# Hybrid encoder: the first two tiles of the first feed-forward layer, fed and ordered differently

## Chip, cores, metric

The kernel runs on one core of one Trainium2 chip. The metric is the device time of one execution in microseconds, the median of the runs. TensorE multiplies, ScalarE, VectorE and GpSimd work on elements, SP issues most transfers; ScalarE and GpSimd issue some too.

## The reference, cut to what matters

Two layers of an encoder over x of 512 tokens x 1024 features. Each layer is a half-step feed-forward block, a mixer with three kinds of attention, and a second feed-forward block; a norm follows at the end. All data is float32. The change touches only the very beginning: the first block's normalised input, multiplied by the gate and up weights.

```
h = rms_norm(x, norm_g[l, 0])
x = x + 0.5 * swiglu(h, ffn_w_gate[l, 0], ffn_w_up[l, 0], ffn_w_down[l, 0])
def swiglu(h, w_gate, w_up, w_down):
    return (jax.nn.silu(h @ w_gate) * (h @ w_up)) @ w_down
```

## The kernel before, in words

Features lie on the 128 partitions: x comes as 8 chunks (k = 0 to 7) of 128 features x 512 tokens. Each operand of a product is split in two: a high part in the short float32r format (ScalarE casts it) and a low part, the rest (VectorE subtracts). A product of a 128 x 128 weight block and a chunk is then three matmuls of 512 columns: high weight x high x, high weight x low x, low weight x high x. Called `h` and `l` are the two parts of a chunk of x (`parts`), `whi` and `wlo` those of a weight tile of 128 x 1024. The gain of the norm is applied in `parts`; the factor 1/rms comes later: `square` adds up the squares in `acc`, `sums` adds them over the partitions (L156) and takes the power -1/2 on GpSimd (`rs`), `finish` spreads `rs` over the partitions (L164), and `gated` multiplies by it when an accumulator is read.

Elsewhere a weight tile is loaded whole (L81), cast (L82), subtracted (L83) and multiplied (L96, L97, L99). The first two tiles of gate and two of up (n = 0 to 3: gate, up, gate, up) are the function `opening`: no data has come yet, so it works on x and the weights chunk by chunk as they land, with four accumulators (three `mm`, one `av`). Before the change the weights came in pieces of 256 columns of one tile (128 KB each), on SP, ScalarE's and GpSimd's queues, then cast (L324) and subtracted (L325); for each chunk all four tiles' two products with high weights followed (L343, L344). After the last chunk the squares were taken, and the 32 low products (L352) came at the end, with `sums` after the second tile and `finish` after the third. The order on each engine is made by a scheduler from the code's order, buffers and its own estimates; the engines work through it strictly in order, and semaphores (DMAHW for SP's and ScalarE's transfers, DMASW for GpSimd's) make them wait.

Of the kernel before, what the change touches and what calls it, by code (L numbers as in the profile page):

```python
# [33 lines left out]
def encoder(ctx: ExitStack, tc: tile.TileContext, a: dict, out: bass.AP):  # L34
# [3 lines left out]
    nc = tc.nc  # L38
# [3 lines left out]
    wpool = ctx.enter_context(tc.tile_pool(name="wpool", bufs=4))  # L42
    work = ctx.enter_context(tc.tile_pool(name="work", bufs=4))
# [4 lines left out]
    def f(ap):  # L48
        return ap.bitcast(F32)
# [39 lines left out]
    def st_tile():  # L89
        return psum.tile([P, S], F32, tag="t", name="st", bufs=2)  # L90
# [213 lines left out]
    def opening(l, i, h, fp, ghi, glo):  # L304

        ws = [
            (wpool.tile([P, 1024], F32R, tag="whi", name="whi"), wpool.tile([P, 1024], F32R, tag="wlo", name="wlo"))
            for _ in range(4)
        ]
        ps = [mm_tile(), mm_tile(), mm_tile(), psum.tile([P, S], F32, tag="av", name="av", bufs=1)]  # L310
        xs = [None] * KC
        raws = [wpool.tile([P, 1024], F32, tag="raw", name="raw", bufs=3) for _ in range(3)]
        raws.append(fp.tile([P, 1024], F32, tag="raw4", name="raw4"))

        def load(k, queue):
            xs[k] = fp.tile([P, S], F32, tag=f"xf{k}", name="xf")
            queue.dma_start(xs[k], a["xT"][k])

        def fetch(n, w, queue):
            queue.dma_start(raws[n][:, w], a["w_gu"][l, i, n // 2, n % 2][:, w])  # L320

        def part(n, w):
            (hi, lo), raw = ws[n], raws[n]
            nc.scalar.copy(hi[:, w], raw[:, w])  # L324
            nc.vector.tensor_tensor(out=lo[:, w], in0=raw[:, w], in1=f(hi[:, w]), op=ALU.subtract)  # L325

        pairs = [slice(k * P, (k + 2) * P) for k in range(0, KC, 2)]
# [588 lines left out]
    h = Norm(0, gain(0, 0))  # L916
    for l in range(DEPTH):
# [4 lines left out]
        if l + 1 < DEPTH:  # L922
            h = Norm(3 * l + 3, gain(l + 1, 0))
# [91 lines left out]
```

## Time and profile before

| | us |
|---|---|
| median of 3 runs | 2483.62 (2482.66 to 2483.65) |
| the profiled execution | 2485.75 |
| its span on the core | 2484.0 |
| TensorE busy in the span | 2465.3 |

The profiled execution is one run by itself, with 1.75 us around its span; its rows give durations, and a sum made with them is set against its own time. Rows of a timeline give the start within the span, the duration, the engine (`PE` TensorE, `PEld` its weight loads, `ACT` ScalarE, `DVE` VectorE, `POOL` GpSimd, `SPq` the issuing of SP), the line and the tiles. Matmul rows overlap: the distance of two starts is the cost, not the duration printed.

### The profile page before, as it was taken

What the parts mean: (1) busy time and instruction counts of PE and PEld (TensorE: products, weight loads), DVE (VectorE), ACT (ScalarE), POOL (GpSimd) and SP (SyncE); (2) the same over time, 40 slices, a digit from 0 to 9 for tenths busy, and PEclk for the clock granted to TensorE, in tenths of its full rate; (3) what the DMA queues carried; (4) which work ended last, traced back from release to release, by engine and by line L of the source; (5) the groups of instructions that cost most, each with busy time, mean ns of one, the idle gap of its engine ahead of it and who ended that gap; (6) DMA issues with size and microseconds to landing.
All of it is one profiled execution on the core that took longest, in us unless ns stands there. A gap on an engine that the chain in (4) does not pass through costs nothing.

```text
span 2484.0 us, 30196 instructions
## 1 busy us (share of the span) xinstructions
PE 2465.3 (99%) x11604; PEld 2054.7 (83%) x11604; DVE 1294.3 (52%) x2178; ACT 1053.8 (42%) x1776; POOL 193.1 (8%) x300
## 2 busy tenths in 40 slices
PE   8999999999999999999999999999999999999998
PEld 7888888888888888888888888888888888888887
DVE  5444335766666644443344443367676766444432
ACT  5333225755557433332232332267555664333322
POOL 2000003311000000000000000033110001000000
PEclk9999999999999999999999999999999999999999
DMA  5323344432322342233432324443322224332232
GB/s 169 102 94 100 119 131 127 118 103 78 93 85 86 124 128 97 95 98 119 133 107 94 101 91 131 140 118 107 98 86 92 86 83 148 119 115 93 95 100 68
DMA packets 80655, 265.24 MB, mean 107 GB/s; under 512 B 10904, under 2 KB 16328, under 8 KB 80512
## 3 DMA queue, kind: packets, MB, share of 16 engines
q1 hardware_dynamic: 67680, 226.59, 29.4%
q0 software_dynamic: 11680, 34.86, 4.9%
q8 instruction: 92, 1.51, 0.2%
q10 hardware_dynamic: 1152, 1.86, 0.2%
q14 instruction: 51, 0.42, 0.1%
HBM read 241.22 MB, written 12.62 MB: 102 GB/s over the span
## 4 chain that ended last, share of the span: by engine, by line
PE 97%; DVE 1%; ACT 1%; issue 0%; DMA 0%; SPq 0%; POOLq 0%; POOL 0%; ACTq 0%; DVEq 0%
PE mm L96 22%; PE mm L97 22%; PE mm L99 22%; PE mm L288 5%; PE mm L290 5%; PE mm L287 5%; PE av L597 2%; PE t L587 1%; PE s L542 1%; PE s L543 1%; PE av L698 1%; PE mm L492 1%; PE mm L491 1%; PE mm L389 1%; PE mm L387 1%; PE mm L388 1%
## 5 line engine op out<-in xcount | busy, mean ns | idle before, releaser
L96 PE MATMUL mm<-h,whi 128*128 128x512 f32 x2112 | 831.7, 394 | 0.2
L97 PE MATMUL mm<-l,whi 128*128 128x512 f32 x2112 | 825.0, 391 | 0.0
L82 ACT CAST whi<-raw 128x1024 fp32r<-128x1024 f32 (+1 forms) x414 | 429.9, 1039 | 715.3 <-PE mm L97 372.7
L83 DVE TENSOR_TENSOR wlo<-raw,whi 128x1024 fp32r<-128x1024 f32 (+1 forms) x414 | 500.6, 1209 | 294.3 <-ACT whi L82 179.7
L99 PE MATMUL mm<-h,wlo 128*128 128x512 f32 x2112 | 521.8, 390 | 0.0
L99 PEld LDWEIGHTS mm<-h,wlo 128*128 128x128 f32 x2112 | 396.7, 188 | 82.2
L96 PEld LDWEIGHTS mm<-h,whi 128*128 128x128 f32 x2112 | 397.0, 188 | 80.7 <-issue 0.8
L97 PEld LDWEIGHTS mm<-l,whi 128*128 128x128 f32 x2112 | 397.3, 188 | 79.4
L298 DVE TENSOR_TENSOR un<-mm,rb 128x512 f32<-128x512 f32 x87 | 60.1, 691 | 296.8 <-PE mm L99 296.8
L288 PE MATMUL mm<-g,whi 128*128 128x512 f32 x528 | 205.7, 390 | 0.0
L287 PE MATMUL mm<-g,whi 128*128 128x512 f32 x528 | 205.6, 389 | 0.0
L106 ACT CAST g<-un 128x512 fp32r<-128x512 f32 x88 | 54.5, 620 | 251.4 <-DVE un L299 251.4
L290 PE MATMUL mm<-g,wlo 128*128 128x512 f32 x528 | 131.4, 390 | 0.0
L295 DVE TENSOR_TENSOR gn<-mm,rb 128x512 f32<-128x512 f32 x88 | 60.8, 691 | 133.4 <-PE mm L99 133.4
L556 ACT ACTIVATE lg<-lg,negm 128x256 f32<-128x256 f32 (+1 forms) x192 | 114.0, 594 | 25.2 <-DVE negm L553 23.7
L61 POOL DMA_DIRECT2D d_x<-x x40 | 22.1, 553 | 1262.9 <-DVE x L246 1262.6
L288 PEld LDWEIGHTS mm<-g,whi 128*128 128x128 f32 x528 | 99.2, 188 | 20.5
L290 PEld LDWEIGHTS mm<-g,wlo 128*128 128x128 f32 x528 | 99.2, 188 | 20.5
L287 PEld LDWEIGHTS mm<-g,whi 128*128 128x128 f32 x528 | 99.1, 188 | 20.5
L296 ACT ACTIVATE gn<-gn 128x512 f32<-128x512 f32 x88 | 55.8, 634 | 123.6 <-DVE gn L295 123.6
L108 DVE TENSOR_TENSOR g<-un,g 128x512 fp32r<-128x512 f32 x88 | 60.9, 692 | 62.8 <-ACT g L106 62.8
L246 DVE SCALAR_TENSOR_TENSOR x<-mm,x 128x512 f32<-128x512 f32 x40 | 27.7, 692 | 109.1 <-PE mm L290 72.4
(223 smaller groups left out, 3037.8 us busy)
## 6 DMA issues: line engine op xcount, KB each, us to landing
raw<-in_w_gu SPq DMA_DIRECT2D x172, 512.0 KB, 3.4
raw<-in_w_down SPq DMA_DIRECT2D x48, 512.0 KB, 3.5
raw<-in_w_gate SPq DMA_DIRECT2D x48, 512.0 KB, 3.5
raw<-in_w_qk SPq DMA_DIRECT2D x44, 512.0 KB, 3.6
raw<-in_w_branch SPq DMA_DIRECT2D x24, 512.0 KB, 3.5
raw<-in_w_last SPq DMA_DIRECT2D x22, 512.0 KB, 3.5
d_x<-x POOLq DMA_DIRECT2D x40, 256.0 KB, 2.4
x<-d_x POOLq DMA_DIRECT2D x40, 256.0 KB, 2.9
```

The lines of the kernel that those rows point to most:

```text
L82: nc.scalar.copy(hi[:, w], raw[:, w])
L83: nc.vector.tensor_tensor(out=lo[:, w], in0=raw[:, w], in1=f(hi[:, w]), op=ALU.subtract)
L96: nc.tensor.matmul(ps, wh, xhi[k], start=k == 0, stop=False)
L97: nc.tensor.matmul(ps, wh, xlo[k], start=False, stop=False)
L99: nc.tensor.matmul(ps, wl, xhi[k], start=False, stop=k == n - 1)
L108: nc.vector.tensor_tensor(out=lo, in0=src, in1=f(hi), op=ALU.subtract)
L287: nc.tensor.matmul(ps, w[k][0], ghi[c + k], start=c + k == 0, stop=False)
L288: nc.tensor.matmul(ps, w[k][0], glo[c + k], start=False, stop=False)
L290: nc.tensor.matmul(ps, w[k][1], ghi[c + k], start=False, stop=c + k == MF - 1)
L295: nc.vector.tensor_tensor(out=gn, in0=pg, in1=h.rb, op=ALU.mult)
L298: nc.vector.tensor_tensor(out=un, in0=pu, in1=h.rb, op=ALU.mult)
L556: nc.scalar.activation(p, p, AF.Exp, bias=negm, scale=-1.0, accum_out=total)
```

## The change

What it does, all of it within `opening`:

- Four matmuls of zeros (a cleared tile, 256 columns, plain float32) stand ahead of everything on TensorE.
- Gate and up weights of a tile pair come in one transfer (`fetch(k, m)`: both of pair m), in pieces of 128 columns for chunk 0 and for chunk 1 and of 256 for chunks 2, 4 and 6, each in a buffer of its own (tag `g`, which the gated outputs use later). The former buffers `raw` are free from the start for the tiles after the opening.
- For the first four chunks the low products come right behind the chunk's high ones; for the last four chunks each tile runs all its products together.
- Squares are taken after every second chunk; `sums` comes after tile 0's last high product and `finish` after tile 1's in the code.

```diff
+        warm = work.tile([P, S], F32, tag="qn", name="warm", bufs=2)
+        nc.vector.memset(warm, 0.0)
+        pw = st_tile()
+        for _ in range(4):
+            nc.tensor.matmul(pw[:, :256], warm[:, :P], warm[:, :256], start=True, stop=True)
+        pieces = {0: slice(0, P), 1: slice(P, 2 * P), 2: slice(2 * P, 4 * P), 4: slice(4 * P, 6 * P), 6: slice(6 * P, D)}
...
-        def fetch(n, w, queue):
-            queue.dma_start(raws[n][:, w], a["w_gu"][l, i, n // 2, n % 2][:, w])
+        def fetch(k, m, queue):
+            w = pieces[k]
+            t = fp.tile([P, S], F32, tag="g", name="piece", bufs=2 * MF)
+            raws[k, m] = t[:, : 2 * (w.stop - w.start)].rearrange("p (a c) -> p a c", a=2)
+            queue.dma_start(raws[k, m], a["w_gu"][l, i, m][:, :, w].rearrange("a p c -> p a c"))
...
-        for j, w in enumerate(pairs):
-            load(2 * j, nc.sync)
-            fetch(0, w, nc.sync)
-            fetch(1, w, nc.sync)
-            fetch(2, w, nc.scalar if j == 0 else nc.gpsimd)
-            fetch(3, w, nc.scalar if j == 0 else nc.gpsimd)
-            load(2 * j + 1, nc.gpsimd)
+        load(0, nc.sync)
+        fetch(0, 0, nc.sync)
+        fetch(0, 1, nc.scalar)
+        load(1, nc.sync)
+        fetch(1, 0, nc.sync)
+        fetch(1, 1, nc.gpsimd)
+        for k in (2, 4, 6):
+            load(k, nc.sync)
+            fetch(k, 0, nc.sync)
+            fetch(k, 1, nc.gpsimd)
+            load(k + 1, nc.gpsimd)
         make_identity(nc, ident)
         for k in range(KC):
             h.parts(k, xs[k])
-            if k % 2 == 0:
+            if k in pieces:
+                part(k)
+            if k < 4:
                 for n in range(4):
-                    part(n, pairs[k // 2])
-            for n in range(4):
-                wk = slice(k * P, (k + 1) * P)
-                nc.tensor.matmul(ps[n], ws[n][0][:, wk], h.hi[k], start=k == 0, stop=False)
-                nc.tensor.matmul(ps[n], ws[n][0][:, wk], h.lo[k], start=False, stop=False)
+                    high(n, k)
+                for n in range(4):
+                    low(n, k)
+            if k % 2:
+                h.square(k - 1, xs[k - 1])
+                h.square(k, xs[k])
         table_loads()
         small_loads()
-        for k in range(KC):
-            h.square(k, xs[k])
         for n in range(4):
-            for k in range(KC):
-                wk = slice(k * P, (k + 1) * P)
-                nc.tensor.matmul(ps[n], ws[n][1][:, wk], h.hi[k], start=False, stop=k == KC - 1)
+            for k in range(4, KC):
+                high(n, k)
+            if n == 0:
+                h.sums()
             if n == 1:
-                h.sums()
-            if n == 2:
                 h.finish()
+            for k in range(4, KC):
+                low(n, k)
```

`part(k)` casts the four tiles' pieces on ScalarE, then subtracts the four on VectorE; `high` and `low` are the matmuls. The call `load(k + 1, nc.gpsimd)` stands behind `fetch(1, 1, nc.gpsimd)` in the code, but in the built order GpSimd's queue has x3, x5 and x7 first, then the up half of piece 1, then those of pieces 2, 4 and 6.

How the order moves, at three places.

ScalarE at the very beginning. `h0`, `h1`, `h2` are the high parts of chunks of x (lines L125), `whi` the high parts of the weights; numbers behind a name tell buffers apart. Before:

```order
L125 ACTIVATE h0_146<-xf_110,ng_75 128x512 [waits DMAHW1_49,DMAHW0_49]
L324 CAST whi_94<-raw_106 128x256 [waits DMAHW2_49]
L324 CAST whi_96<-raw_107 128x256 [waits DMAHW3_49]
L324 CAST whi_98<-raw_108 128x256 [waits DMAHW5_49]
L125 ACTIVATE h1_166<-xf_116,ng_75 128x512 [waits DMASW0_49]
L324 CAST whi_100<-raw4_109 128x256 [waits DMAHW6_49]
L125 ACTIVATE h2_178<-xf_118,ng_75 128x512 [waits DMAHW4_49]
```

Now (`acc` is the square of chunk 0, which is not needed until later):

```order
L125 ACTIVATE h0_153<-xf_113,ng_75 128x512 [waits DMAHW1_49,DMAHW0_49]
L337 CAST whi_94<-piece_115 128x128 [waits DMAHW2_49]
L337 CAST whi_96<-piece_115 128x128
L133 ACTIVATE acc_201<-xf_113 128x512
L125 ACTIVATE h1_177<-xf_119,ng_75 128x512 [waits DMAHW3_49]
L337 CAST whi_98<-piece_117 128x128 [waits DMAHW4_49]
L337 CAST whi_100<-piece_117 128x128
L337 CAST whi_94<-piece_121 128x128 [waits DMAHW5_49]
L337 CAST whi_96<-piece_121 128x128
L337 CAST whi_98<-piece_123 128x128 [waits DMASW3_49]
L337 CAST whi_100<-piece_123 128x128
```

The casts of tiles 2 and 3 for chunk 0 (`whi_98`, `whi_100` from `piece_117`) stand behind the conversion of chunk 1 now, which waits for that chunk's transfer (DMAHW3); before, tile 1's cast and tile 2's stood ahead of it.

SP's transfers, which one queue carries in this order. `xf` is a chunk of x, `raw` and `piece` are weights; `raw_402` and on are whole tiles for the stage after the opening. Before:

```order
L317 DMA xf_118<-in_xT 128x512
L320 DMA raw_106<-in_w_gu 128x256
L320 DMA raw_107<-in_w_gu 128x256 [waits DMAHW0_49]
L317 DMA xf_126<-in_xT 128x512 [waits DMAHW1_49]
L320 DMA raw_106<-in_w_gu 128x256 [waits DMAHW2_49]
L320 DMA raw_107<-in_w_gu 128x256 [waits DMAHW3_49]
L317 DMA xf_134<-in_xT 128x512 [waits DMAHW4_49]
L320 DMA raw_106<-in_w_gu 128x256 [waits DMAHW5_49]
L320 DMA raw_107<-in_w_gu 128x256 [waits DMAHW6_49]
L81 DMA raw_387<-in_w_gu 128x1024 [waits DMAHW5_49,DMAHW7_49,DMAHW2_49,DVE_49]
L81 DMA raw_393<-in_w_gu 128x1024 [waits DMAHW3_49,DMAHW6_49,DMAHW0_49,DVE_49]
```

Now:

```order
L325 DMA xf_119<-in_xT 128x512
L331 DMA piece_121<-in_w_gu 128x2x128
L325 DMA xf_125<-in_xT 128x512
L331 DMA piece_127<-in_w_gu 128x2x256
L325 DMA xf_133<-in_xT 128x512 [waits DMAHW0_49]
L331 DMA piece_135<-in_w_gu 128x2x256 [waits DMAHW1_49]
L325 DMA xf_141<-in_xT 128x512 [waits DMAHW2_49]
L81 DMA raw_402<-in_w_gu 128x1024 [waits DMAHW3_49]
L81 DMA raw_408<-in_w_gu 128x1024 [waits DMAHW4_49]
L81 DMA raw_474<-in_w_gu 128x1024 [waits DMAHW5_49]
L331 DMA piece_143<-in_w_gu 128x2x256 [waits DMAHW6_49]
L81 DMA raw_480<-in_w_gu 128x1024 [waits DMAHW7_49,DMAHW3_49,DVE_49]
```

The last piece (`piece_143`, chunks 6 and 7 of the first gate and up tiles) stands behind three whole tiles of 512 KB now; each row waits for an earlier transfer's semaphore, this one for that of the third chunk of x.

TensorE between the sums of squares (L156) and the spread (L164). `wlo` marks low products, `whi` high ones. Before:

```order
L156 MATMUL st_337<-ones_78,acc_296 128x1 [waits DVE_49]
L156 MATMUL st_337<-ones_78,acc_296 128x1 x3
L352 MATMUL mm_104<-h0_146,wlo_99 128x512
L352 MATMUL mm_104<-h1_166,wlo_99 128x512
L352 MATMUL mm_104<-h2_178,wlo_99 128x512
L352 MATMUL mm_104<-h3_198,wlo_99 128x512
L352 MATMUL mm_104<-h4_210,wlo_99 128x512
L352 MATMUL mm_104<-h5_230,wlo_99 128x512
L352 MATMUL mm_104<-h6_242,wlo_99 128x512
L352 MATMUL mm_104<-h7_262,wlo_99 128x512
L164 MATMUL st_352<-ident_77,rs_335 128x128 [waits Pool_49]
L164 MATMUL st_352<-ident_77,rs_335 128x128 x3
```

Now:

```order
L156 MATMUL st_328<-ones_78,acc_201 128x1 [waits DVE_49]
L156 MATMUL st_328<-ones_78,acc_201 128x1 x3
L344 MATMUL mm_104<-h4_252,whi_98 128x512
L345 MATMUL mm_104<-l4_254,whi_98 128x512
L164 MATMUL st_347<-ident_77,rs_326 128x128 [waits PE_49,Pool_49]
L164 MATMUL st_347<-ident_77,rs_326 128x128 x3
L344 MATMUL mm_104<-h5_264,whi_98 128x512
L345 MATMUL mm_104<-l5_266,whi_98 128x512
```

Eight low products stood between the sums and the spread, which waits for GpSimd's `rs`; now two products of the third tile stand there, and the rest of that tile comes behind the spread.

## Rows read from the trace of the kernel before

**Rows 1.** The page: engines' busy time (share of the span), number of instructions.

```profile
PE 2465.3 (99%) x11604; PEld 2054.7 (83%) x11604; DVE 1294.3 (52%) x2178; ACT 1053.8 (42%) x1776; POOL 193.1 (8%) x300
```

**Rows 2.** Waits of TensorE, whole program: waited for, us in total, times, longest.

```profile
PE mm L343 <- ACT whi L324: 7.8, 2, 4.9
```

**Rows 3.** Timeline of the opening: start us, us, engine, line, operation [idle before].

```profile
0.85 0.07 DVE L69 MEMSET nhalf<- 128x8 f32 x1
...
3.85 0.72 ACT L125 ACTIVATE h<-xf,ng 128x512 fp32r<-128x512 f32 x1 [1.15 <-DMA ng<-in_norm_g]
...
4.60 0.75 DVE L127 SCALAR_TENSOR_TENSOR l<-xf,ng,h 128x512 fp32r<-128x512 f32 x1 [3.69 <-ACT h L125]
...
4.91 0.79 PE L343 MATMUL mm<-h,whi 128*128 128x512 f32 x1 [4.91 <-ACT whi L324]
...
9.10 0.80 PE L343 MATMUL mm<-h,whi 128*128 128x512 f32 x1 [2.90 <-ACT whi L324]
```

**Rows 4.** Chain that ended last, 0 to 40 us: start us, us, what.

```profile
1.66 6.96 DMA raw<-in_w_gu
...
9.90 0.43 PE mm L344
...
13.74 0.43 PE mm L343
...
25.83 3.63 PE mm L352 x16
29.46 0.79 PE st L156 x8
30.25 1.97 PE mm L352 x8
32.22 0.47 PE st L164 x4
```

**Rows 5.** DMA issues at 1.26 to 1.4 us: count, KB each, us to landing.

```profile
raw<-in_w_gu SPq DMA_DIRECT2D x1, 128.0 KB, 3.0
```

**Rows 6.** DMA issues at 1.71 to 1.8 us.

```profile
raw<-in_w_gu SPq DMA_DIRECT2D x1, 128.0 KB, 7.0
```

**Rows 7.** Timeline: SP's fourth transfer, then its fifth and sixth.

```profile
2.13 0.43 SPq L317 DMA_DIRECT2D xf<-in_xT  x1
...
2.61 1.56 SPq L320 DMA_DIRECT2D raw<-in_w_gu  x2
```

**Rows 8.** Windows: us, busy us of each engine, clock column, DMA share, GB/s.

```profile
2.00:15.00 13.00, 7.18 (x18) 5.25 (x19) 6.23 (x13) 6.92 (x16) 9.10 (x19) 1.00 1.00 333
```

**Rows 9.** DMA issues at 2.55 to 2.9 us: SP's fourth and fifth transfer.

```profile
xf<-in_xT SPq DMA_DIRECT2D x1, 256.0 KB, 7.7
...
raw<-in_w_gu SPq DMA_DIRECT2D x1, 128.0 KB, 8.7
```

**Rows 10.** Chain, 66 to 70 us: two float32 matmuls of 512 columns.

```profile
67.22 1.83 PE st L192 x4
```

**Rows 11.** Instruction groups by line, 0 to 62 us: count, busy us, mean ns.

```profile
L324 ACT CAST whi<-raw 128x256 fp32r<-128x256 f32 x16 | 5.6, 400 | 5.5 <-DMA raw<-in_w_gu 5.5
```

**Rows 12.** Timeline around sums and spread, and the first row of the next stage.

```profile
29.55 1.23 DVE L83 TENSOR_TENSOR wlo<-raw,whi 128x1024 fp32r<-128x1024 f32 x1 [0.59 <-PE mm L352]
...
30.70 0.15 DVE L157 TENSOR_SCALAR rt<-st 128x4 f32<-128x4 f32 x1
30.94 1.04 POOL L158 TENSOR_TENSOR rs<-rt,nhalf 128x4 f32<-128x4 f32 x1 [11.82 <-DVE rt L157]
...
34.38 0.39 PE L96 MATMUL mm<-h,whi 128*128 128x512 f32 x1
```

**Rows 13.** DMA queues from 5 to 14 us: packets, MB, share.

```profile
DMA packets 1847, 3.18 MB, mean 353 GB/s; under 512 B 306, under 2 KB 1075, under 8 KB 1847
...
q0 software_dynamic: 549, 1.62, 52.2%
q1 hardware_dynamic: 1209, 1.48, 48.3%
```

More of the change, by code (lines that the diff above doesn't have):

```diff
@@ L310, in opening @@
         ps = [mm_tile(), mm_tile(), mm_tile(), psum.tile([P, S], F32, tag="av", name="av", bufs=1)]
-        xs = [None] * KC
-        raws = [wpool.tile([P, 1024], F32, tag="raw", name="raw", bufs=3) for _ in range(3)]
-        raws.append(fp.tile([P, 1024], F32, tag="raw4", name="raw4"))
+        xs, raws = [None] * KC, {}
+        warm = work.tile([P, S], F32, tag="qn", name="warm", bufs=2)
[4 more added lines that the diff above has]
+        pieces = {0: slice(0, P), 1: slice(P, 2 * P), 2: slice(2 * P, 4 * P), 4: slice(4 * P, 6 * P), 6: slice(6 * P, D)}
         def load(k, queue):
@@ L317, in load, with part, high, low @@
             queue.dma_start(xs[k], a["xT"][k])
-        def fetch(n, w, queue):
-            queue.dma_start(raws[n][:, w], a["w_gu"][l, i, n // 2, n % 2][:, w])
[L322 to L327, printed above, removed]
-        for j, w in enumerate(pairs):
-            load(2 * j, nc.sync)
-            fetch(0, w, nc.sync)
-            fetch(1, w, nc.sync)
-            fetch(2, w, nc.scalar if j == 0 else nc.gpsimd)
-            fetch(3, w, nc.scalar if j == 0 else nc.gpsimd)
-            load(2 * j + 1, nc.gpsimd)
+        def fetch(k, m, queue):
[3 more added lines that the diff above has]
+            queue.dma_start(raws[k, m], a["w_gu"][l, i, m][:, :, w].rearrange("a p c -> p a c"))
+        def part(k):
+            w = pieces[k]
+            for n in range(4):
+                hi, raw = ws[n][0], raws[k, n // 2][:, n % 2]
+                nc.scalar.copy(hi[:, w], raw)
+            for n in range(4):
+                (hi, lo), raw = ws[n], raws[k, n // 2][:, n % 2]
+                nc.vector.tensor_tensor(out=lo[:, w], in0=raw, in1=f(hi[:, w]), op=ALU.subtract)
+        def high(n, k):
+            wk = slice(k * P, (k + 1) * P)
+            nc.tensor.matmul(ps[n], ws[n][0][:, wk], h.hi[k], start=k == 0, stop=False)
+            nc.tensor.matmul(ps[n], ws[n][0][:, wk], h.lo[k], start=False, stop=False)
+        def low(n, k):
+            nc.tensor.matmul(ps[n], ws[n][1][:, k * P : (k + 1) * P], h.hi[k], start=False, stop=k == KC - 1)
+        load(0, nc.sync)
[9 more added lines that the diff above has]
+            load(k + 1, nc.gpsimd)
         make_identity(nc, ident)
@@ L337, in opening @@
             h.parts(k, xs[k])
-            if k % 2 == 0:
+            if k in pieces:
+                part(k)
+            if k < 4:
                 for n in range(4):
-                    part(n, pairs[k // 2])
-            for n in range(4):
-                wk = slice(k * P, (k + 1) * P)
-                nc.tensor.matmul(ps[n], ws[n][0][:, wk], h.hi[k], start=k == 0, stop=False)
-                nc.tensor.matmul(ps[n], ws[n][0][:, wk], h.lo[k], start=False, stop=False)
+                    high(n, k)
+                for n in range(4):
+                    low(n, k)
+            if k % 2:
+                h.square(k - 1, xs[k - 1])
+                h.square(k, xs[k])
         table_loads()
         small_loads()
-        for k in range(KC):
-            h.square(k, xs[k])
         for n in range(4):
-            for k in range(KC):
-                wk = slice(k * P, (k + 1) * P)
-                nc.tensor.matmul(ps[n], ws[n][1][:, wk], h.hi[k], start=False, stop=k == KC - 1)
+            for k in range(4, KC):
+                high(n, k)
+            if n == 0:
+                h.sums()
             if n == 1:
-                h.sums()
-            if n == 2:
                 h.finish()
+            for k in range(4, KC):
+                low(n, k)
         gated(h, fp, ps[0], ps[1], ghi, glo)
```

## Prediction

> **What bounds the kernel now.** I read the page first: TensorE is busy 2465.3 us of the span, 99% [rows 1], so only waits of TensorE, or extra work on it, can move the time. The waits of TensorE over the whole program come next: the one that matters is in the opening, 7.8 us in two pieces for the cast `whi` of ScalarE [rows 2]. So I read the opening row by row. The first 4.91 us have no matmul; two matmuls run, then nothing until 9.10 [rows 3]. The chain says what that is: the transfer of the second weight tile, 1.66 to 8.62 [rows 4]. From 9.90 on the chain has matmuls 0.43 us apart until about 14.2, 11 of them, and then 0.227 apart (16 in 3.63) [rows 4]. 512 columns in 0.43 us is the 1.2 GHz level, in 0.227 us the 2.4 GHz level (with a little on top); the clock column of the windows view prints 1.00 over this stretch [rows 8], so the spacing is the row to trust. After 14.2 TensorE never waits in the opening, and the next stage (L96) begins at 34.4 [rows 12].
>
> A floor: the opening has 96 matmuls, 96 x 0.227 = 21.8 us, plus the sums of squares 0.79 and the spread 0.47 [rows 4]: 23.1 us. Started at 4.91 and never held up it would end at 28.0. The whole change can therefore give 6.4 us at most, 0.26% of the time. Under 0.2% (5.0 us) faster or slower I call it the same, about what a measurement of this kernel can tell.
>
> **The change, part by part.**
>
> *Zeros.* Four matmuls of 256 columns in plain float32. The rows of L192 are two such matmuls of 512 columns, four passes in 1.83 us at the high level [rows 10], 0.457 a pass; eight passes of 256 columns are 1.83 us there, 3.66 at 1.2 GHz. They can start when VectorE has cleared the tile, at 0.9 [rows 3] plus a clear that I put between nothing and the 0.75 us of a 512-column VectorE operation [rows 3]: they run from about 1.3 to 5.0 at the low level. The first real matmul was at 4.91 anyway. Cost 0, at most 0.4 us, and that lies inside the wait below. What they may give is the clock: before, matmuls had run without a pause for 4.9 us (9.10 to about 14.1) when it rose. Zeros and the first real products together are about 5.5 us without a pause, so I expect the high level by the time the bulk begins. Lost to the low level before: 11 x (0.43 - 0.227) = 2.2 us.
>
> *Loads.* Now SP's queue carries x0, piece 0 (gate), x1, piece 1, x2, piece 2, x4, piece 4, x6, then three 512 KB weight loads, then piece 6. ScalarE issues the up half of piece 0. GpSimd issues x3, x5, x7 first, then the up halves of pieces 1 and on. The first two transfers of a queue land 3.0 us after issue [rows 5]; SP's third took 7.0 [rows 6], its fourth and fifth, issued at 2.13 and 2.61 [rows 7], took 7.7 and 8.7 [rows 9]: so landings at 8.62, 9.8 and 11.3, after 512, 768 and 896 KB of that queue. I carry this over by bytes in SP's queue, since the transfer engines are full at 333 GB/s from 2 to 15 us [rows 8] and stay so. x0 and both halves of piece 0 land as x0 and the first pieces did, by about 4.5. x1 ends at 640 KB: between 8.62 and 9.8, I take 9.2. Piece 1 ends at 768 KB but in 256 runs instead of 128: between 9.8 and 11.3; I take 11.3, because the runs get shorter.
>
> *What TensorE does with that.* The ScalarE order decides: the conversion of x1 stands ahead of the casts of the up half of piece 0. So chunk 0 goes in two parts. Gate tiles, five matmuls, from about 5.1 to 7. Then ScalarE waits for x1 (9.2), converts it (0.72 [rows 3]), casts 128 columns (I take 0.3, between half and the whole of the 0.40 of 256 columns [rows 11]) and at about 10.2 the remaining seven matmuls run, 1.6 us, to 11.8. Chunk 1 needs piece 1: 11.3 + 0.3 + a release of 0.1 = 11.7. So chunk 1 begins at **11.8**, with 12 of 96 matmuls done. From there nothing is missing: chunks 1 to 3 are 36 matmuls, 8.2 us, and x2, piece 2 lie 256 KB apart, 0.8 us each at 333 GB/s. What is missing could be piece 6, behind three 512 KB loads: 4.3 MB passed by 15 us [rows 8]; the 1.6 MB more take 4.7 us and half a us to be signalled, so it lands at about 20.2 (19.5 at the 353 GB/s of 5 to 14 us [rows 13]; 22 with 2 us of it, as SP's third shows). It is needed 40 matmuls after 11.8, at 20.9. It just arrives.
>
> *Low parts at once.* The same 32 products in another order: 0 by themselves. Their worth is only that TensorE has 12 and not 8 products per chunk while the loads come; counted in the 84 products that remain.
>
> *Sums and spread.* Before, eight low products stood between L156 and L164; now two. The path from the end of L156 to L164 is 30.25 to 32.22 on the chain [rows 4], with rt at 30.70 and the power on GpSimd 30.94, 1.04 long [rows 12]; rt began when VectorE's 1.23 us subtraction from 29.55 let go [rows 12], so the bare path is 1.4 to 1.9 us. Two products cover 0.45. A new wait of TensorE: 0.9 to 1.4 us, I take **1.2**. Queued behind it is everything on TensorE. The last addition to `acc` now stands behind a weight subtraction on VectorE that waits for the first tile's last product; that takes about 2.2 us (1.23 + 0.69 and releases) and 12 products of the second tile, 2.7 us, cover it.
>
> *Squares earlier, gated output earlier.* Hidden: ScalarE was busy 6.9 and VectorE 6.2 of the 13 us from 2 to 15 [rows 8]; without that room each of the eight squares and seven additions would put up to 0.75 us of its engine [rows 3] ahead of a cast or a subtraction. The next stage's accumulators free themselves while the last two tiles run.
>
> **Sum.** 11.8 + 84 x 0.227 (19.1) + 0.79 + 0.47 + 1.2 = 33.4. By piece 6 instead, with 0.5 for its cast: 20.2 + 0.5 + 44 x 0.227 (10.0) + 2.5 = 33.2, just less. Against 34.4: **1.0 us less**. The profiled execution took 2485.75 with a span of 2484.0; it becomes 2484.7. That execution lies 2.1 us above the median of 2483.62, so the forecast is 2482.6. The rest of the program stands in the same order on every engine, so nothing is added later.
>
> **A rule against it.** Between 5 and 14 us GpSimd's queue moved 1.62 MB in 549 packets, SP's 1.48 MB in 1209 [rows 13]: 2.9 KB a packet against 1.2 KB. The Trainium skill, "DMA: Bandwidth & Descriptors", section on queues, rings and completion order, says that each transfer engine takes turns between queues packet by packet, so a queue with shorter runs gets the smaller part while the other has work. The trace agrees so far that the queue of small packets needed more than twice as many for fewer bytes; no run here shows 512-byte runs. What it would do here is rival 4, worked out from the landings.
>
> **Rivals.**
> 1. *Clean stream.* SP's queue gets an even half of 333 GB/s from 2.0 on, and a landing is signalled 1 us after the bytes: 640 KB by 5.9, 768 KB by 6.7, so x1 lands at 6.9 and piece 1 at 7.7. For it: the 3.0 us of the first transfers [rows 5], and the total bytes allow it. Against: every transfer of SP behind 384 KB took 7 us or more [rows 6, 9]. The rest of chunk 0 then runs from 7.9 to 9.5 and chunk 1 begins there: 9.5 + 21.6 = 31.1. Piece 6, with the 353 GB/s of 5 to 14 us throughout, lands at 19.0 and holds the end to 32.0: 2481.2.
> 2. *The clock does not stay up.* After the five matmuls TensorE is idle some 3 us, as it was before 9.10 [rows 3]. If the low level holds for the next 12 or so, seven matmuls take 3.0 instead of 1.6, and five more lose 0.2 each: chunk 1 at 13.2, end 35.8, **slower** by 1.4 us, 2485.0. It decides against the change once chunk 1's full-rate work begins after 12.8 (34.4 - 21.6). For it: the half rate after the gap at 9.10 [rows 3, 4]. Against: there the clock had not risen yet. The skill's "TensorE: Matmul & The Clock Gate", part 1, has both halves: sustained work lifts the clock, idling drops it; no row here shows a drop.
> 3. *Piece 6 late.* It is the one piece moved behind 1.5 MB. Each us after 20.9 adds one; it takes the result past no change at 21.9, and past 0.2% only at 26.9. For it: SP's issue of it waits for x2. Against: the bytes above. At 23 the end is 35.5, 2484.7; at 27, 2488.7.
> 4. *The short runs eat the gain.* From SP's fourth landing to its fifth 128 KB took 1.5 us (9.8 to 11.3). If halving the runs costs piece 1 between half a step and a whole one more, it lands at 12.1 to 12.8, chunk 1 begins at 12.5 to 13.2 and the end is 34.1 to 34.8: no change, 2483.6. For it: the packet sizes [rows 13]. Against: GpSimd's queue has little left by then.
>
> **How the numbers follow.** Forecast 0.45 (end 32.4 to 34.4, 2481.6 to 2483.6), clean stream 0.2 (and 0.03 of it below 2478.7), low clock 0.15, late piece 6 0.08 (0.03 past 2488.6), short runs 0.12. The range leaves out a tenth on each side: 2480.0 to 2485.4. Faster by over 0.2%: 0.04; within: 0.92; slower: 0.04.
>
> **What the profile after would show.** Right: five matmuls by 7, then a gap that ends when x1 lands near 9.2; chunk 1 at 11.8 spaced 0.227; a wait of TensorE for `rs` of about 1.2 us at L164; L96 begins at 33.4; span 2483. Wrong: matmuls spaced 0.43 after 10; a gap at k = 6 for the cast of piece 6; x1 landing before 7.5; no wait at L164. I would be wrong past 0.2% if the opening ends before 29.4 or after 39.4.

## The result and the profile after

The kernel after takes 2487.85 us (median of 22 runs, 2486.01 to 2489.58). The kernel before, run beside it, takes 2483.55 (22 runs, 2482.40 to 2484.83). The ratio is 1.0018, 95% interval 1.0012 to 1.0024: 4.3 us slower. The forecast was 2482.6, 1 us faster, with a range up to 2485.4. The difference is within 0.2%, but to the other side, and the time is outside the range.

The profiled execution of the kernel after took 2486.89 with a span of 2485.1, against 2485.75 and 2484.0 before. Where the two part is quickly found: the next stage (L96) begins at 34.99 instead of 34.38 [rows 12], and from there to the end it is 2450.1 us after and 2449.6 before. Of the 1.1 us between the two executions 0.6 lie in the opening and 0.5 behind it; the stretch behind it took 2449.6 to 2450.3 in all fourteen profiles of this case that keep its order, so I look for the cause in the opening. The page's busy time of TensorE, 2466.5 against 2465.3 [rows 1], has the zeros in it.

The waits of TensorE over the whole program, kernel after (us in total, times, longest), answer to [rows 2]:

```profile
PE mm L344 <- ACT whi L337: 3.9, 2, 2.1
PE st L164 <- POOL rs L158: 1.7, 1, 1.7
PE st L318 <- DVE warm L315: 1.5, 1, 1.5
```

The casts still stop it, for 3.9 us instead of 7.8, and a wait for `rs` is new. The timeline of the kernel after has the places. First the start, which answers to [rows 3]:

```profile
1.52 3.56 PE L318 MATMUL st<-warm 128*128 128x256 f32 x8 [1.52 <-DVE warm L315]
...
4.88 0.49 PE L344 MATMUL mm<-h,whi 128*128 128x512 f32 x1
...
6.28 0.40 PE L348 MATMUL mm<-h,wlo 128*128 128x512 f32 x1
...
7.83 0.72 ACT L125 ACTIVATE h<-xf,ng 128x512 fp32r<-128x512 f32 x1 [2.27 <-DMA xf<-in_xT]
...
8.79 0.50 PE L344 MATMUL mm<-h,whi 128*128 128x512 f32 x1 [2.11 <-ACT whi L337]
...
10.28 0.39 PE L348 MATMUL av<-h,wlo 128*128 128x512 f32 x1
10.38 0.38 SPq L331 DMA_DIRECT2D piece<-in_w_gu  x1
10.51 0.39 PE L344 MATMUL mm<-h,whi 128*128 128x512 f32 x1
```

This is the forecast's picture, only earlier: zeros, five products, a gap until x1 lands (7.8), the other seven, and chunk 1 from 10.51 (forecast 11.8), all 0.23 us apart. The row of SP at 10.38 is the one to keep in mind: it issues piece 6. Its landing, from the DMA issues of 10.3 to 10.45 us (count, KB, us to landing):

```profile
piece<-in_w_gu SPq DMA_DIRECT2D x1, 256.0 KB, 10.3
```

So piece 6 lands at 20.7. The same timeline, around chunk 6 of the first tile:

```profile
19.37 0.39 PE L345 MATMUL mm<-l,whi 128*128 128x512 f32 x1
19.97 0.61 ACT L136 ACTIVATE sq<-xf 128x512 f32<-128x512 f32 x1
20.49 1.92 ACT L337 CAST whi<-piece 128x256 fp32r<-128x256 f32 x6
...
21.54 0.50 PE L344 MATMUL mm<-h,whi 128*128 128x512 f32 x1 [1.78 <-ACT whi L337]
```

TensorE had reached chunk 6 at 19.6 and went on at 21.54. And around the sums, which answers to [rows 12]:

```profile
27.20 0.16 DVE L157 TENSOR_SCALAR rt<-st 128x4 f32<-128x4 f32 x1 [0.92 <-PE st L156]
27.27 1.23 DVE L83 TENSOR_TENSOR wlo<-raw,whi 128x1024 fp32r<-128x1024 f32 x1
...
27.45 1.97 POOL L158 TENSOR_TENSOR rs<-rt,nhalf 128x4 f32<-128x4 f32 x1 [6.93 <-DVE rt L157]
...
29.46 0.65 PE L164 MATMUL st<-ident,rs 128*128 128x128 f32 x4 [1.73 <-POOL rs L158]
...
34.99 0.39 PE L96 MATMUL mm<-h,whi 128*128 128x512 f32 x1
```

GpSimd's power takes 1.97 here and took 1.04 before. The windows view (columns as in [rows 8]) shows how full the other engines are while TensorE runs toward chunk 6:

```profile
15.00:20.00 5.00, 4.76 (x21) 3.59 (x20) 4.90 (x9) 5.00 (x11) 3.23 (x7) 1.00 1.01 327
```

The columns are TensorE, its weight loads, VectorE, ScalarE, GpSimd: ScalarE has no free time at all from 15 to 20 us, VectorE 0.1.

### The profile page after: what moved, and what is told of

The parts are those of the page before. It is cut to its first block, busy times and chain, and to the rows that moved or that the text cites. A ratio compares the mean times of both kernels' runs of the same rounds, so it can differ in the third digit from the quotient of the medians.

```text
span 2485.1 us, 30211 instructions
## 1 busy us (share of the span) xinstructions
PE 2466.5 (99%) x11612; PEld 2053.7 (83%) x11612; DVE 1294.6 (52%) x2183; ACT 1054.0 (42%) x1780; POOL 193.0 (8%) x297
## 3 DMA queue, kind: packets, MB, share of 16 engines
q10 hardware_dynamic: 1136, 1.73, 0.2%
## 4 chain that ended last, share of the span: by engine, by line
PE 96%; DVE 1%; issue 1%; ACT 1%; POOL 0%; DMA 0%; POOLq 0%; ACTq 0%; DVEq 0%
PE mm L96 22%; PE mm L99 22%; PE mm L97 22%; PE mm L290 5%; PE mm L288 5%; PE mm L287 5%; PE av L625 2%; PE t L615 1%; PE s L570 1%; PE s L571 1%; PE av L726 1%; PE mm L519 1%; PE mm L520 1%; PE mm L416 1%; PE mm L415 1%
## 5 line engine op out<-in xcount | busy, mean ns | idle before, releaser
L96 PE MATMUL mm<-h,whi 128*128 128x512 f32 x2112 | 830.9, 393 | 0.2
L96 PEld LDWEIGHTS mm<-h,whi 128*128 128x128 f32 x2112 | 396.8, 188 | 81.0 <-issue 0.8
L61 POOL DMA_DIRECT2D d_x<-x x40 | 22.2, 555 | 1265.5 <-DVE x L246 1265.5
L287 PEld LDWEIGHTS mm<-g,whi 128*128 128x128 f32 x528 | 99.1, 188 | 20.5
L290 PEld LDWEIGHTS mm<-g,wlo 128*128 128x128 f32 x528 | 99.1, 188 | 20.5
```

The lines of the kernel that those rows point to most:

```text
L96: nc.tensor.matmul(ps, wh, xhi[k], start=k == 0, stop=False)
L287: nc.tensor.matmul(ps, w[k][0], ghi[c + k], start=c + k == 0, stop=False)
L290: nc.tensor.matmul(ps, w[k][1], ghi[c + k], start=False, stop=c + k == MF - 1)
```

## The experiments

Fifteen runs follow, two of them of the kernels as they are, each of 11 executions beside the kernel before on the same chip. Ratios are to that kernel. Edits are shown against the kernel after, if nothing else is said.

**The two kernels once more.** The account above leaves a question: the profiles differ by 1.1 us, the medians by 4.3. `before_again` is the kernel before and `after_again` the kernel after, without an edit.

> The kernel before, unchanged, profiled again. Theory A (the first profiled execution of the kernel before was an unlucky one: its second weight tile landed at 8.62 us, and an ordinary one is about 2 us shorter): median 2483.6, and if this profile is near the median, the first stage after the opening (L96) begins near 32.2 instead of 34.4, with the second group of matmuls starting near 6.7 instead of 9.1. Theory C (the opening is as profiled and the 4.3 us are lost in the rest of the program): L96 begins at 34.4 again and the span from there to the end is shorter than the 2449.6 us of the first profile by 2 us.

> The changed kernel, unchanged, profiled again. Theory A: median 2487.8; its three waits of TensorE (for the up half of piece 0 about 2.1 us, for piece 6 about 1.8, for rs about 1.7) are there again, L96 begins at 35 to 36.5. Theory B (in ordinary executions the clock falls to the low level in the gap between the two parts of chunk 0, and the first profile happened to miss it): matmuls spaced 0.43 us for 2 to 5 us somewhere between 9 and 20, mean granted clock 0.998 or less, L96 at 36 or later. Theory C: L96 at 35.0 and the rest longer by 1 us or more than in the first profile of this kernel (2450.1).

`before_again`: 2483.49 (2482.68 to 2484.26), ratio 1.0000 (0.9991 to 1.0009). Its profiled execution is an ordinary one, 2483.52. Timeline of this second profile of the kernel before:

```profile
5.14 0.80 PE L343 MATMUL mm<-h,whi 128*128 128x512 f32 x1 [5.14 <-ACT whi L324]
5.73 0.69 PE L344 MATMUL mm<-l,whi 128*128 128x512 f32 x1
6.79 0.80 PE L343 MATMUL mm<-h,whi 128*128 128x512 f32 x1 [0.36 <-ACT whi L324]
...
10.80 0.63 PE L344 MATMUL mm<-l,whi 128*128 128x512 f32 x1
...
31.86 0.40 PE L96 MATMUL mm<-h,whi 128*128 128x512 f32 x1
```

The transfer that took 7.0 us in the profile ahead of the prediction [rows 4, 6] took 4.7 here, so the gap to 9.10 [rows 3] ends at 6.79, the 2.4 GHz level is there by 11.6 instead of about 14.2, and L96 begins at 31.86, 2.5 us earlier. The rest is the same, 2449.9. **The opening that I measured the change against had one late transfer.** In the four other profiles with the old loads (`before_zeros`, `old_loads` and its two variants below) the same transfer took 4.2 to 4.4. Its row in `before_again`, from the DMA issues at 1.66 us:

```profile
raw<-in_w_gu SPq DMA_DIRECT2D x1, 128.0 KB, 4.7
```

`after_again`: 2486.64 (2486.15 to 2489.58), ratio 1.0015 (1.0007 to 1.0024). In its profile (2486.47) no transfer is late: five products from 5.57, x1 at 7.1, and yet piece 6 (landing 20.5) leaves TensorE without work from 18.88 to 20.99 and `rs` until 28.91; L96 begins at 34.42. Profile against ordinary profile the change costs 2.6 us in the opening. Of theory A the waits for piece 6 and `rs` are there again; the clock does not fall in this profile, but five of the eleven runs take 2488.12 to 2489.58, apart from the other six (2486.15 to 2486.64).

**One part of the change undone, or done alone.**

`no_zeros`: the five lines of `warm` are left out.

> The changed kernel without the four matmuls of zeros. If the zeros buy the high clock early: the first 5 and the next 7 products run 0.43 apart, about 2.5 us lost at the low level, of which the wait for piece 6 hides up to 1.8: +0.7 to +2.5 us against the changed kernel, 2488.5 to 2490.5. If theory B is true and the zeros only lift a clock that falls again: 0 to +0.7, 2487.8 to 2488.5.

2485.42 (2484.83 to 2487.81), ratio 1.0009 (1.0000 to 1.0018). The first products are at the low level until 8.5, but chunk 6 is reached at 18.7 all the same and waits until 21.03. Both branches of the expectation had it slower than the kernel after; it is 1.2 us faster. In this build seven products stand between L156 and L164 instead of two, so I put the gain down to the missing wait for `rs`, not to the missing zeros; this run alone does not separate the two. Its windows (same columns; the last three are clock, DMA share, GB/s):

```profile
19.00:22.00 3.00, 0.97 (x4) 0.84 (x5) 3.00 (x8) 2.46 (x8) 0.85 (x2) 1.00 0.62 118
22.20:29.00 6.80, 6.80 (x23) 5.35 (x22) 3.34 (x11) 1.16 (x2) 1.05 (x1) 0.50 0.26 81
29.20:35.00 5.80, 5.80 (x28) 4.82 (x27) 4.22 (x6) 3.58 (x5) 0.00 (x0) 1.00 0.28 90
```

After the wait the granted clock is 0.50, the 1.2 GHz level, from 22.2 to 29, with TensorE busy throughout: 23 matmuls in 6.8 us, where the next 5.8 us at 2.4 GHz hold 28. This execution is the longest of the eleven.

`squares_end`: squares behind the last chunk, sums and spread one tile later, as they were before.

```diff
-            if k % 2:
-                h.square(k - 1, xs[k - 1])
-                h.square(k, xs[k])
+        for k in range(KC):
+            h.square(k, xs[k])
...
-            if n == 0:
+            if n == 1:
                 h.sums()
-            if n == 1:
+            if n == 2:
                 h.finish()
```

> The changed kernel with the squares taken after the last chunk, sums after the second tile and finish after the third, as before the change. Two waits are attacked: the one for rs (1.7 us, since eight products of a tile stand between again) and the casts of piece 6 that stood behind squares on ScalarE, busy 5.00 of 5.00 us from 15 to 20. If these are what the change lost: 1.5 to 2.5 us less than the changed kernel, 2485.3 to 2486.3. If the squares only fill ScalarE's time beside the late piece 6 and rs is hidden anyway: less than 0.7 us, 2487.1 or more.

2485.66 (2484.18 to 2486.45), ratio 1.0008 (0.9999 to 1.0017). No wait for `rs`, but the wait for piece 6 is longer, 18.43 to 20.95, with ScalarE not full (4.43 of 5.00 us): the squares are not what delays the casts of piece 6, its landing at 20.3 is. So the time lies where the first theory put it, but only the wait for `rs` went. Here too the clock falls after the wait (window of this kernel):

```profile
22.00:25.00 3.00, 3.00 (x9) 2.32 (x8) 2.98 (x7) 1.81 (x3) 0.00 (x0) 0.50 0.01 3
```

`finish_later`: only the second half of that diff.

> The changed kernel with the sums after the second tile's products and the spread after the third's, as before; loads, zeros and squares as changed. Theory, the wait for rs is a loss of its own: the 1.7 to 2.1 us at L164 go, the wait at chunk 6 stays at 1.8 to 2.7, and the time falls by 1.5 to 2.1, to 2484.6 to 2485.1 (runs in which the clock falls after chunk 6 stay above). Rival, the wait is only moved (VectorE's subtractions or the release of the accumulators wait instead): the time stays at 2486.6 within 0.4.

2485.91 (2484.80 to 2486.60), ratio 1.0011 (1.0002 to 1.0020). The runs fall into two groups: five at a mean granted clock of 0.999 with 2484.80 to 2485.27, and six at 0.998 with 2485.91 to 2486.60. In the profile, one of the second group, the wait for piece 6 (18.63 to 20.71) is followed by this window:

```profile
21.00:24.00 3.00, 3.00 (x8) 2.33 (x8) 2.25 (x6) 2.15 (x4) 0.00 (x0) 0.50 0.09 18
```

Between runs of 0.999 clock `finish_later` is 1.3 us under `after_again` (lowest 2484.80 against 2486.15), or about 1.1 with the kernel before on each chip (2482.92, 2483.20) taken off; its wait at L164 is 0.34 instead of 1.73. The wait for `rs` is a loss of its own, of about that size.

`before_zeros`: the kernel before with the five lines of `warm` ahead, and nothing else.

> The kernel before with nothing but the four multiplications of zeros added ahead. Theory, zeros lift the clock where nothing else bounds: the 8 to 10 products that ran 0.43 apart from 6.8 on run 0.227 apart, 1.5 to 1.9 us less, L96 at about 30.2 and 2481.4 to 2482.0. Rival, the pieces' landings bound the first chunks as soon as the products are quick: waits for whi appear between 8 and 14 us, and the time is 2483 to 2483.6, as before.

2483.03 (2482.39 to 2483.32), ratio 1.0000 (0.9991 to 1.0009). The rival holds. Timeline of this kernel:

```profile
6.49 0.50 PE L348 MATMUL mm<-h,whi 128*128 128x512 f32 x1 [0.91 <-ACT whi L329]
6.83 0.40 PE L349 MATMUL mm<-l,whi 128*128 128x512 f32 x1
...
10.58 0.50 PE L348 MATMUL mm<-h,whi 128*128 128x512 f32 x1 [0.35 <-ACT whi L329]
...
12.01 0.50 PE L348 MATMUL mm<-h,whi 128*128 128x512 f32 x1 [0.70 <-ACT whi L329]
```

The products are quick from 6.8 on; at 10.58 and 12.01 they wait for casts that wait for pieces, and at 14.04 for a low part of x. L96 begins at 31.73 against 31.86. In the old order the low level cost nothing: its time lay inside the landings.

**Piece 6.** `piece6_raw` puts both halves of the last piece into a buffer of the whole tiles, `combined` does so together with the edit of `squares_end`.

```diff
+            if k == 6 and m == 0:
+                both[0] = wpool.tile([P, 1024], F32, tag="raw", name="raw", bufs=3)
+            t = both[0][:, m * S : (m + 1) * S] if k == 6 else fp.tile([P, S], F32, tag="g", name="piece", bufs=2 * MF)
-            t = fp.tile([P, S], F32, tag="g", name="piece", bufs=2 * MF)
```

> Both halves of the last piece (chunks 6 and 7) go into one of the three buffers of the whole weight tiles, so that their transfer is issued ahead of the whole tiles and one whole tile fewer is loaded early; nothing else is edited. (The built order lets more products stand between L156 and L164: seven instead of two.) Theory, the piece behind three whole tiles is the loss: no wait of TensorE at chunk 6 (1.8 to 2.7 us in the changed kernel), so the clock does not fall afterwards in any run, the wait for rs shrinks from 1.7-2.1 to about 0.6, L96 begins near 31.5 and the time is 2483.0 to 2484.0, that of the kernel before. Rival, the transfers as a whole are late (the same bytes, halved runs), or ScalarE full of squares delays the casts: a wait of 1.5 us or more for whi stays at chunks 4 to 6, and the time stays at 2485.5 or above.

> The changed kernel with the last piece in a buffer of the whole tiles, the squares after the last chunk, sums after the second and spread after the third tile. By the theory that the three losses (piece 6, rs, ScalarE filled with squares) are all there is: no wait after chunk 1 begins near 10, L96 at 30.4 to 31.2, 2482.0 to 2482.8, about 1 us under the kernel before. Rival, a further loss lies in the loads (halved runs, one piece of 128 columns first): waits for whi between 10 and 18 us, and no better than 2483.5.

`piece6_raw`: 2486.45 (2485.58 to 2486.94), ratio 1.0013 (1.0005 to 1.0022). `combined`: 2487.90 (2486.10 to 2489.89), ratio 1.0020 (1.0011 to 1.0029). Both went against the theory. SP did issue piece 6 early (6.0), but the edit also moved its up half to the third place in GpSimd's queue, behind two chunks of x and ahead of the up halves of the earlier pieces. Timeline of `combined`:

```profile
2.50 0.74 POOL L333 DMA_DIRECT2D raw<-in_w_gu  x1
...
7.36 0.71 POOL L333 DMA_DIRECT2D piece<-in_w_gu  x1 [2.87 <-issue]
```

The second row is the up half of the piece for chunks 2 and 3. GpSimd issues it only after a pause of 2.87 us, it takes 6.8 to land, at 14.2, and TensorE waits for it from 12.5 to 14.66. A wait at chunk 6 had become one at chunk 2. So neither run tested the theory.

`piece6_own` keeps every queue but SP's in its order: the gate half of the last piece alone gets a buffer of its own, `piece6_own_finish` adds the later sums and spread of `finish_later`.

```diff
-            t = fp.tile([P, S], F32, tag="g", name="piece", bufs=2 * MF)
+            tag = "g" if (k, m) != (6, 0) else "g60"
+            t = fp.tile([P, S], F32, tag=tag, name="piece", bufs=2 * MF if tag == "g" else 1)
```

> The changed kernel with one edit: the gate half of the last piece gets a buffer of its own, so that SP issues it right behind x6 and ahead of the three whole tiles; GpSimd's queue keeps its order (seven products instead of two then stand between L156 and L164). Theory, the piece behind the whole tiles is what the change lost: it lands near 16 instead of 20.5, TensorE does not wait at chunk 6, the clock does not fall, the wait for rs shrinks to about 0.9, L96 begins at 30.6 to 31.2 and the time is 2482.6 to 2483.4. Rival, the up halves in GpSimd's queue, which compete with the whole tiles, are as late: waits of 1 us or more at chunks 2 to 6, and the time is 2485 or more.

> The same, with the sums after the second and the spread after the third tile as well. Theory, piece 6 and rs were the two losses: no wait of TensorE of over 0.5 us from 10 us on, L96 at 29.8 to 30.3, time 2481.7 to 2482.5, about 1 us under the kernel before. Rival, the opening is bound by its bytes: 2483.2 or more, with waits for whi.

`piece6_own`: 2483.96 (2483.67 to 2484.59), ratio 1.0003 (0.9995 to 1.0012). `piece6_own_finish`: 2484.18 (2483.29 to 2484.82), ratio 1.0003 (0.9994 to 1.0012). The DMA issues of `piece6_own` at 6.7 us, and its timeline:

```profile
piece<-in_w_gu SPq DMA_DIRECT2D x1, 256.0 KB, 8.2
```

```profile
20.88 0.40 PE L346 MATMUL mm<-l,whi 128*128 128x512 f32 x1
21.55 0.75 DVE L127 SCALAR_TENSOR_TENSOR l<-xf,ng,h 128x512 fp32r<-128x512 f32 x1
...
22.35 0.50 PE L346 MATMUL mm<-l,whi 128*128 128x512 f32 x1 [1.07 <-DVE l L127]
...
31.96 0.39 PE L96 MATMUL mm<-h,whi 128*128 128x512 f32 x1
```

The gate half lands at 15.0, TensorE does not wait for a piece after 10 us, the runs lie within 0.9 us (11 of 11 at a clock of 0.999) where those of the kernel after spread over 3.6, and L96 begins at 31.96. Two lines of buffer choice give back 2.8 us: 2486.64 is 3.4 over the kernel before on its chip (2483.20), 2483.96 is 0.7 over it (2483.29). The slowest of its eleven runs is 1.4 us under the fastest of all 33 of the kernel after. Not all of it is piece 6: the build also puts seven products between L156 and L164, and L164 does not wait. Piece 6 by itself is priced by the pair `finish_later` and `piece6_own_finish`, whose code differs in these two lines alone and which have little or no wait for `rs` (0.34 and none): 3.0 and 0.9 us over the kernel before on their chips, so 2.1 us, 1.3 if only the runs of `finish_later` at a clock of 0.999 are taken; the rest is the fall of the clock. What is left in its place is a wait of 1.07 for the low part of the last chunk, which stands behind six weight subtractions on VectorE. By the expectation it should have been 2482.6 to 2483.4; I put the difference down to that wait, which is not shown: `own_late` below is without it and no faster. Moving the spread on top of it changes nothing, since there is no wait for `rs` any more; the 2481.7 to 2482.5 that the theory named are missed by 1.7 us.

**What is left to gain.** `old_loads` is the kernel before with only the order of the products changed; `old_loads_zeros` adds the zeros. Against the kernel before:

```diff
-                nc.tensor.matmul(ps[n], ws[n][0][:, wk], h.hi[k], start=k == 0, stop=False)
-                nc.tensor.matmul(ps[n], ws[n][0][:, wk], h.lo[k], start=False, stop=False)
+            if k < 4:
+                for n in range(4):
+                    high(n, k)
+                for n in range(4):
+                    low(n, k)
...
         for n in range(4):
-            for k in range(KC):
-                wk = slice(k * P, (k + 1) * P)
-                nc.tensor.matmul(ps[n], ws[n][1][:, wk], h.hi[k], start=False, stop=k == KC - 1)
+            for k in range(4, KC):
+                high(n, k)
             if n == 1:
                 h.sums()
             if n == 2:
                 h.finish()
+            for k in range(4, KC):
+                low(n, k)
```

> The kernel before with nothing but the new order of the products (low products of chunks 0 to 3 at once, the rest tile by tile); loads, squares, sums and spread at their old places, no zeros. Theory, the order of the products is worth nothing by itself, since TensorE never waited after 7 us: 2483.0 to 2483.9, L96 at 31.7 to 32.1. Rival, the order is part of the loss (a wait for rs, or for a subtraction of VectorE that now stands ahead): 2484.5 or more.

> The whole change except its loads: old loads, new order of the products, and the zeros. In the kernel before, zeros alone gave nothing, since the quicker products waited for pieces between 10 and 14 us. Theory, the low products fill those waits, so that here the zeros give the 1.7 us of the low level back: L96 at 30.0 to 30.5, 2481.5 to 2482.2, which would put the whole loss on the loads. Rival, the pieces bound in any order of the products: 2483.0 or more.

`old_loads`: 2484.44 (2483.70 to 2486.65), ratio 1.0006 (0.9997 to 1.0015), half a microsecond over the forecast, with a new wait of 0.6 at L156. `old_loads_zeros`: 2487.75 (2483.95 to 2489.24), ratio 1.0017 (1.0008 to 1.0026), as slow as the whole change without having its loads. Its timeline, and its windows:

```profile
24.37 0.39 PE L334 MATMUL mm<-h,whi 128*128 128x512 f32 x1
...
26.64 0.69 DVE L137 TENSOR_TENSOR acc<-acc,sq 128x512 f32<-128x512 f32 x1
27.38 1.87 PE L156 MATMUL st<-ones,acc 128*128 128x1 f32 x8 [2.62 <-DVE acc L137]
```

```profile
27.20:33.90 6.70, 6.52 (x21) 5.59 (x22) 1.72 (x7) 1.42 (x2) 1.04 (x1) 0.50 0.45 150
```

Now the sums of squares are late: with the low products pulled forward, TensorE comes to L156 earlier than the eight squares and seven additions are done, waits 2.6 us, and then runs at the 1.2 GHz level until 33.9. Neither theory nor rival had this.

`old_loads_zeros_late` moves the sums and the spread one more tile back (`n == 2`, `n == 3`). `own_late` does the same to `piece6_own` with the squares at the end, `own_late_no_zeros` is that without the zeros.

> The kernel with the old loads, the new order of the products and the zeros, and with the sums after the third and the spread after the fourth tile's high products (in the run before, the sums stood a tile earlier and waited 3.0 us for the last square, after which the clock fell). Theory, the squares of ScalarE were the only thing that the quicker TensorE ran into: no wait at L156, no fall of the clock, L96 at 29.8 to 31, 2481.8 to 2482.8, and a spread of the runs under 1.5 us. Rival, pieces or the gated output bind instead: 2483.3 or more.

> The changed kernel with the gate half of the last piece in a buffer of its own, the squares after the last chunk, sums after the third and spread after the fourth tile. (Chunk 7's low part of x then stands ahead of the last subtractions on VectorE.) Theory, the last loss of the run with a buffer of its own was the 1.4 us that TensorE waited for that low part at chunk 7: no wait from 10 us on, L96 at 30 to 31, 2482.0 to 2483.0. Rival, the up half of piece 6, which lands near 16.8 from GpSimd's queue, binds anyway, and squares ahead of its casts on ScalarE make it later: a wait for whi at the second half's tiles, 2484 or more.

> The same without the zeros. Theory, with every later wait gone the zeros are worth what the first nine or ten products lose at the low level: 1.5 to 2.0 us slower than with them. Rival, chunks 1 to 3 wait for pieces anyway, so zeros are worth nothing here either: equal within 0.4.

2483.46 (2482.17 to 2484.66), 2483.73 (2482.71 to 2484.27) and 2483.25 (2482.67 to 2484.62); ratios 1.0001 (0.9992 to 1.0010), 1.0001 (0.9993 to 1.0010) and 1.0000 (0.9992 to 1.0009). All runs of all three are at a clock of 0.999. The large waits are gone, and none is better than the kernel before. The first lies where its rival put it, the second between theory and rival. The zeros are worth nothing here either: without them the median is 0.5 us lower, within the scatter of the runs. Timeline of `own_late`:

```profile
25.64 1.05 PE L156 MATMUL st<-ones,acc 128*128 128x1 f32 x8 [0.64 <-DVE acc L137]
...
28.28 1.22 DVE L83 TENSOR_TENSOR wlo<-raw,whi 128x1024 fp32r<-128x1024 f32 x1
28.45 1.96 POOL L158 TENSOR_TENSOR rs<-rt,nhalf 128x4 f32<-128x4 f32 x1 [8.77 <-DVE rt L157]
...
30.46 0.65 PE L164 MATMUL st<-ident,rs 128*128 128x128 f32 x4 [0.91 <-POOL rs L158]
...
34.03 0.19 PEld L96 LDWEIGHTS mm<-h,whi 128*128 128x128 f32 x1 [1.05 <-DVE gn L295]
```

TensorE still waits for the squares, for `rs`, and at L96 for the gated output that has to release an accumulator. (L96 is late by the two L192 matmuls of 1.83 us as well, which this build runs earlier; the rest after it is 2448.0.) Where loads no longer held TensorE up (`old_loads`, `old_loads_zeros`, `own_late`), the path over squares, sums, spread and gate, which runs on ScalarE, VectorE and GpSimd, was next.

## Why the prediction was wrong

**The base.** The step that failed first is "Against 34.4": the opening was compared with one in which a transfer was late, and then "that execution lies 2.1 us above the median, so the forecast is 2482.6" was applied to the changed kernel too. Those 2.1 us were that late transfer: 7.0 us from issue to landing, against 4.2 to 4.7 in the five other profiles with these loads, and an opening 2.5 us longer than in `before_again`, in an execution 2.2 us longer. An ordinary opening before ends at 31.86, and even the forecast end of 33.4 is 1.5 us later than that. With everything else as forecast the answer was slower, 2485.0. The clue lay open: a profiled execution above all three runs, with a row of 7.0 us beside one of 3.0 for the same bytes [rows 5, 6].

**Zeros.** Cost nothing, as said, and the 2.4 GHz level was there for the bulk: the first wide run of products is 0.23 apart. What they were to give, 2.2 us, was no loss to begin with: `before_zeros` shows the same end, with waits for pieces in the place of the low level.

**Loads and chunk 1.** x1 landed at 7.8 and piece 1 at 8.9, not 9.2 and 11.3, since the landings carried over came from the same execution with its late transfer; chunk 1 began at 10.51, not 11.8. Rival 1 was nearest here. Rival 4 fell: piece 1 with its 512-byte runs (6.7 us to landing) came well ahead of the 12.1 to 12.8 that this rival needed; what short runs cost by themselves no run here isolates.

**Piece 6, "It just arrives".** The landing was sized well, 20.2 forecast, 20.7 measured (20.5 in the second profile). The need was not: it was counted from 11.8, and TensorE was there at 19.6 (18.9). The 1.3 us won at chunk 1 were lost here, and 0.6 more. That is rival 3, held at 0.08, and it needed no late piece but an early TensorE. `piece6_own` shows it: the same bytes in another place of SP's queue, and the wait is gone; the pair `finish_later` and `piece6_own_finish` prices it at 2.1 us with the fall of the clock.

**Rival 2, at another place.** The low level did not come in the first gap but after the wait at chunk 6. It is shown where a profile caught it (`no_zeros`, `squares_end`, `finish_later`: 0.50 after a wait of 2.1 to 2.5 us). In the kernel after itself no profile did, after waits of 1.9 and 2.1; its runs say it: 9 of 22 at a mean clock of 0.999 with 2486.01 to 2488.10, 13 lower with 2487.56 to 2489.58. That these 13 fell at the same place is argued, not shown. The Trainium skill, "TensorE: Matmul & The Clock Gate", part 1, has the rule that idling drops the clock; in that these windows agree, and the prediction had no row that showed it.

**Sums and spread.** The wait was forecast as 1.2 and measured 1.73, since GpSimd's power took 1.97 instead of the 1.04 taken from [rows 12]. `finish_later` prices it at 1.1 to 1.3 us.

**Squares, "Hidden".** The room was counted from 2 to 15 us [rows 8], but all squares except the first run from 10.6 to 23 and the last addition starts at 25.3, and from 15 to 20 ScalarE is full. In the kernel after they cost nothing that is shown (in `squares_end` the wait for piece 6 stays without them), because piece 6 is later still; without it they are the next bound (`old_loads_zeros`, `own_late`).

The sum with what was measured: 33.4 - 1.3 (chunk 1) + 1.9 (piece 6: 2.17 from product to product, less 0.23) + 0.5 (`rs`) = 34.5, against 34.99; the remaining half is the products right behind L156, L164 and the wait at 21.54, which follow at 0.32 to 0.34 instead of 0.23, and the wait for `rs`, which is 1.89 from product to product. Against 31.86 it is 3.1 us; the medians' 4.3 hold the runs with the lower clock.

## What to carry to other kernels

Before a sum is set against one profiled execution, see where that execution lies among the runs: what makes it long must not be taken from the other side of the sum. When the start of a chain gets earlier, recompute when each later transfer is needed, and look first at the transfer that stands behind bulk loads that a freed buffer now lets go early. And where engines share the work of a stage, a saving on one is worth at most the distance to the next path: here the zeros ran into the landings of the pieces (`before_zeros`), the early low products into the sums of squares (`old_loads`, `old_loads_zeros`).

## What the runs showed of the hardware

GpSimd's power of 128x4 took 1.04 to 1.05 us in 13 profiles and 1.96 or 1.97 in four (the kernel after twice, `finish_later`, `own_late`): those four in which a subtraction of VectorE over 1024 columns (1.22 or 1.23 us) was already running when it began, as in the rows of `own_late` above. Where that subtraction began behind it, the power stayed at 1.04 to 1.05, as in the timeline of `own_late_no_zeros`:

```profile
27.75 1.05 POOL L158 TENSOR_TENSOR rs<-rt,nhalf 128x4 f32<-128x4 f32 x1 [7.58 <-DVE rt L157]
...
27.94 1.23 DVE L83 TENSOR_TENSOR wlo<-raw,whi 128x1024 fp32r<-128x1024 f32 x1 [0.27 <-issue]
```

The Trainium skill, "SBUF — State Buffer", section "SBUF: two separate sides", says that VectorE and GpSimd share a pair of ports as an exclusive lock, which the one that starts first keeps for its whole instruction. The four long rows agree: in the kernel after the subtraction ends at 28.50 and the power 0.92 later. The other direction does not: in the rows of `own_late_no_zeros` the subtraction took its usual 1.23 beside a power that had begun before it.

The zeros did not always lift the clock. In `old_loads_zeros_late` (timeline) they ran from 1.52 on and the products were still 0.43 apart up to 10.8:

```profile
1.52 3.78 PE L316 MATMUL st<-warm 128*128 128x256 f32 x8 [1.52 <-DVE warm L313]
5.09 0.79 PE L334 MATMUL mm<-h,whi 128*128 128x512 f32 x1
6.38 0.80 PE L334 MATMUL mm<-h,whi 128*128 128x512 f32 x1 [0.49 <-ACT whi L329]
...
9.96 1.05 PE L338 MATMUL mm<-h,wlo 128*128 128x512 f32 x2
```

The products at 5.09 and 6.38 are 1.29 us apart. The kernel after has a longer gap, 6.28 to 8.79, and stays at 0.23. What decides it no run here settles; it also leaves open what the zeros would give this build.

GpSimd pauses between its first issues of transfers and the next one, waiting for nothing that the profile shows: 0.5 to 2.6 us in the six profiles with the old loads, the two of the kernel before at 2.6 and 1.0, 1.1 to 2.6 with the changed loads, and 2.9 and 3.2 in `combined` and `piece6_raw`, whose early issues hold one 256 KB piece more. In these two the transfer put early into its queue pushed another behind the pause. Why it pauses is open.
